# A short-convolution trunk on one core: the seventh small product behind product f, the convolution behind the addition of the sixth, w_out's sums and the small products' operands at other places

## The chip, the cores and the metric

The kernel runs on one core of a Trainium2 chip. The metric is device time in microseconds (us); the median of the runs is compared. The engines named below are PE (matmul), DVE (the vector engine), ACT (the scalar engine), POOL (GpSimd) and SP, whose queue issues nearly all DMAs. Each engine works through its own queue in the order in which the program names its instructions, and waits at the head of that queue until what it needs has been signalled.

## The reference

With DEPTH = 1 only layer 0 runs, the gated short convolution. For x of 1024 positions by 1024 channels:

```
u = rms_norm(x, pre_norm)
z, bg, cg, v = split(u @ w_in, 4)        # w_in: 1024 x 8192, each part 2048 wide
y = bg * causal_dwconv(cg * v, conv_w) * silu(z)     # 3 taps
out = x + rms_norm(y @ w_out, post_norm)             # w_out: 2048 x 1024
```

All of it is float32.

## The kernel before

The kernel computes y transposed, 128 channels of the 2048 at a time: 16 chunks c. A chunk is two pairs of column blocks of w_in: the even pair p = 2c holds (cg, v), the odd pair p = 2c + 1 holds (z, bg). A pair is computed by Strassen's method in a variant of seven products, named a to g, on halves of the 1024 rows of w_in and halves of the 1024 positions. Each product is 12 matmuls of 128 x 128 by 128 x 512: four blocks of rows, and three matmuls for each, because a float32 operand is split into a high part (a cast on ACT, L154) and a low part (a subtraction on DVE, L155), and high by low, low by high and high by high are added. `split_w` makes the two parts of one weight operand. The operands that are sums of weight blocks (c, d, e, f) come from POOL (`add_s`, L142 to L150).

The products a, c, d and g of a pair add into one PSUM bank x; between them the bank is read: by a copy on ACT (`snap`, L196, after a, c and e), or by an addition on DVE into the copy (L215 after d, L220 after f). The next product into the same bank must wait for the read of the one before.

From chunk 2 (DEEP) on, product b of the even and the odd pair is merged with the same method once more: b is made of seven small products a' to g', six matmuls of 128 x 256 each (L684 to L686). a', c', d' and g' share one bank, e' and f' another, and each small product is read by an addition on DVE (`deep_after`, L695). The first four belong to the even pair's stretch and f', d', g' to the odd pair's. Their position operands (c', d', e', g') are sums of blocks of product b's operand; POOL makes them once (`deep_parts`, L614 to L624, called after product f of pair 2) and `deep_split` makes their high and low parts on ACT and DVE. Their weight operands come from `deep_sums` on POOL and `deep_prep`.

The order of the program is one list of slots (L738 to L753): for an odd pair c, f', e, d', d, g', f, a of the next pair, g. For each slot PE's matmuls are issued, then `prepare` issues the splits of those weight operands whose slot begins within 7 us (LEAD) of this one's end by a fixed count of 2.72 us a product and 0.72 a small product, then `after` or `deep_after` issues the reads, then what is tied to the slot (L787 to L827).

The convolution of a chunk needs both halves of cg * v in the tile gpad: the second half is a POOL product after f of the even pair (L225), the first half is a DVE product after the last small product of the even row, f' (`start_conv`, L236). `conv` is a scaled copy on ACT over 1024 positions (L581) and two multiply-adds on DVE (L583). Its output cv is multiplied by the gates: after d (POOL, L217, then L223 after f) and after g (DVE, L229 and L230), which needs the SiLU of z on ACT (L779 after g', L222 after f). `y_done` then stores the chunk to DRAM.

The output projection is a Strassen product as well. Its operands that are sums are made during the first part and stored to DRAM: those of y by `add_y` (DVE, after d of an even pair), those of w_out by `add_t`: four subtractions and four stores, for blocks j = 0 to 6 on DVE in the even pairs 4 to 16, and for j = 7 on POOL in pair 17 (`TODO`, L735). `fetch_t` issues their loads after product c of the same pair. All loads and stores go through SP's queue in program order.

All working tiles of 128 x 512 float32 are pages of one pool of 36.

Of the kernel before, what the change touches and what calls it, by code (L numbers as in the profile page):

```python
# [16 lines left out]
DEEP = 2  # L17
# [4 lines left out]
def kernel(  # L22
# [16 lines left out]
    nc = tc.nc  # L39
# [5 lines left out]
    NC = CI // P  # L45
# [25 lines left out]
    def page(name, dtype=F32, shape=(HB,)):  # L71

        return pages.tile([P, *shape], dtype, tag="pg", name=name, bufs=PAGES)
# [58 lines left out]
    def block(p, n, k):  # L132
        return flat(raws[p, n, k])

    def add_s(p, kinds):

        if p >= len(PAIRS):
            return
        for i in kinds:
            if i == "d":  # L140
                t = block(p, 1, 0)
                nc.gpsimd.tensor_sub(t, block(p, 0, 0), t)  # L142
            else:
                t = page(f"s{i}_{p}")
                if i == "e":
                    nc.gpsimd.tensor_add(t, block(p, 1, 0), block(p, 1, 1))  # L146
                elif i == "c":
                    nc.gpsimd.tensor_sub(t, sums[p, "e"], block(p, 0, 0))  # L148
                else:
                    nc.gpsimd.tensor_sub(t, block(p, 0, 1), sums[p, "c"])  # L150
            sums[p, i] = t

    def split(src, hi, lo):
        nc.scalar.copy(hi, src)  # L154
        nc.vector.tensor_sub(lo, src, hi.bitcast(F32))  # L155
# [21 lines left out]
    def product(p, i, ks=None):  # L177

        w = wt[p, i]
        which = {"b": "y", "e": "v", "f": "v"}.get(i, "x")  # L180
        first = i in "abe"
        if first and (p, which) not in banks:
            banks[p, which] = bank(f"p{which}_{p}")
        ps = banks[p, which]
        for k in range(KH) if ks is None else ks:
            hi, lo = (h[:, k * P : (k + 1) * P] for h in w)
            last = k == KH - 1
            nc.tensor.matmul(ps, lo, UH[i][:, k], start=first and k == 0, stop=False, skip_group_check=True)  # L188
            nc.tensor.matmul(ps, hi, UL[i][:, k], start=False, stop=False, skip_group_check=True)  # L189
            nc.tensor.matmul(ps, hi, UH[i][:, k], start=False, stop=last, skip_group_check=True)  # L190
# [44 lines left out]
    def start_conv(c):  # L235
        nc.vector.tensor_mul(gpad[:, TAPS - 1 : TAPS - 1 + HB], banks[2 * c, "x"], sn[2 * c, "a"])  # L236
        conv(c)
# [8 lines left out]
    def fetch_s(c):  # L246

        if c >= CH:
            ts = [page(f"s{e}_{c}") for e in (0, 1)]
            for e in (0, 1):  # L250
                nc.sync.dma_start(ts[e], y_d[:, c - CH, e * HB : (e + 1) * HB])
            done[c] = done[c], *ts
# [19 lines left out]
    def fetch_t(j):  # L272

        ts[j] = [page(f"t{n}_{j}") for n in range(4)]
        for n, t in enumerate(ts[j]):
            nc.sync.dma_start(t, wov[:, j + n // 2 * CH, n % 2 * HB : (n % 2 + 1) * HB])

    def add_t(j, eng):

        t = ts.pop(j)  # L280
        eng.tensor_sub(t[1], t[1], t[0])
        eng.tensor_sub(t[3], t[3], t[1])
        eng.tensor_sub(t[0], t[3], t[0])
        eng.tensor_sub(t[2], t[2], t[3])
        for n in range(4):
            nc.sync.dma_start(t_d[:, n, j], t[n])
# [341 lines left out]
    def deep_split(i):  # L628

        k0, l0 = DEEP_U[i]  # L630
        ls = slice(l0, l0 + HH)
        if i != "e'":
            deep[i] = [tmp.tile([P, KQ, HH], F32R, tag="ub", name=f"u{i[0]}{h}_deep", bufs=6) for h in "hl"]
        for k in range(KQ):
            if i == "e'":
                hi, lo = UH["b"][:, k, ls], UL["b"][:, k, ls]
            else:
                hi, lo = (t[:, k] for t in deep[i])
            split(deep[k0 + k][:, ls], hi, lo)
# [29 lines left out]
    def deep_product(c, i):  # L669

        n, off = DEEP_W[i]
        which = {"b'": "y'", "e'": "v'", "f'": "v'"}.get(i, "x'")
        first = i in ("a'", "b'", "e'")
        if first:
            banks[c, which] = bank(f"p{which[0]}2_{c}")
        ps = banks[c, which][:, :HH]
        for k in range(KQ):
            hi, lo = (h[:, off + k * P : off + (k + 1) * P] for h in deep_w[c, n])
            if i in deep:
                uh, ul = (t[:, k] for t in deep[i])  # L680
            else:
                kk, l0 = {"a'": (k, 0), "b'": (k + KQ, 0), "e'": (k, HH), "f'": (k + KQ, HH)}[i]
                uh, ul = (u["b"][:, kk, l0 : l0 + HH] for u in (UH, UL))
            nc.tensor.matmul(ps, lo, uh, start=first and k == 0, stop=False, skip_group_check=True)  # L684
            nc.tensor.matmul(ps, hi, ul, start=False, stop=False, skip_group_check=True)
            nc.tensor.matmul(ps, hi, uh, start=False, stop=k == KQ - 1, skip_group_check=True)  # L686
# [5 lines left out]
    def deep_after(c, i):  # L692
        which, row, half = DEEP_C[i]
        t = sn[2 * c + row, "a"][:, half * HH : (half + 1) * HH]
        nc.vector.tensor_add(t, banks[c, which][:, :HH], t)  # L695
        if i == "f'":
            start_conv(c)


# [35 lines left out]
    TODO = {p: p // 2 - 2 for p in range(4, 4 + 2 * CH - 2, 2)}  # L735
# [3 lines left out]
    for p in range(2, len(PAIRS)):  # L739
        q = p + 1  # L740
        more = p // 2 >= DEEP
        sub = {"c": "a'", "e": "b'", "f": "c'", "a": "e'"} if p % 2 == 0 else {"c": "f'", "e": "d'", "d": "g'"}
        for i in "cedf":
            slots.append((i, p))
            if more and i in sub:
                slots.append((sub[i], p // 2))
        if q <= END:
            slots.append(("a", q))
            if more and p % 2 == 0:
                slots.append((sub["a"], p // 2))  # L750
            if q // 2 < DEEP:
                slots.append(("b", q))
        slots.append(("g", p))  # L753


    at, t = [], 0.0
# [6 lines left out]
    def prepare(n):  # L763
        while ready[0] < len(slots) and at[ready[0]] < at[n + 1] + LEAD:
            i, p = slots[ready[0]]
            if i[1:]:
                deep_prep(p, i)
            elif (p, i) not in wt:
                split_w(p, i)
            ready[0] += 1  # L770

    first_chunk("")
    for n, (i, p) in enumerate(slots):
        if i[1:]:
            deep_product(p, i)
            prepare(n)
            deep_after(p, i)
            if i == "g'":
                nc.scalar.activation(sn[2 * p + 1, "a"], sn[2 * p + 1, "a"], AF.Silu)  # L779
            continue  # L780
        product(p, i)
        prepare(n)
        after(p, i)
        q, prev = p + 1, p // 2 - 1
        if p == 2:
            first_chunk(i)
        if i == "c":  # L787
            if p % 2 and p // 2 < DEEP:
                nc.scalar.activation(sn[p, "a"], sn[p, "a"], AF.Silu)
            if p in TODO:  # L790
                fetch_t(TODO[p])
            if p % 2 == 0 and p > 2:
                fetch_s(prev)
            if p % 2 == 0 and p // 2 >= DEEP:
                deep_sums(p // 2, 1)
        elif i == "e":
            add_s(q, "ec")
        elif i == "d":
            if p + 2 <= END:
                fetch(p + 2)  # L800
            add_s(q, "d")
            if p % 2 == 0 and p > 2:
                add_y(prev)
        elif i == "f":
            add_s(q, "f")
            if p == 2:
                add_y(0)
            if p == 2 and DEEP < NC:
                deep_parts()
        elif i == "g":  # L810
            if p in TODO:
                add_t(TODO[p], nc.gpsimd if p % 2 else nc.vector)
            if p % 2 and q <= END and q // 2 >= DEEP:
                deep_sums(q // 2, 0)
            if p == 2 and DEEP < NC:
                deep_split("c'")
                deep_split("e'")
        if p == 3 and DEEP < NC:
            if i == "c":
                deep_split("d'")  # L820
            elif i == "e":
                deep_split("g'")
        if p == END - 1 and i in "cd":
            fetch_unit()
        if p == END and i in "acdg":
            split_unit()
            fetch_unit()  # L827
# [153 lines left out]
```

## Time and profile before

| | |
|---|---|
| median of 3 runs | 816.36 us (816.34 to 816.61) |
| profiled execution | 817.24 us |
| its span (first to last instruction) | 815.3 us |
| mean granted clock of PE | 0.994 |
| busy: PE, DVE, POOL, ACT | 785.2, 645.3, 356.8, 333.1 us |

In the timeline a row is: start, length, engine, line, operation, the tiles written and read, and in square brackets the idle time of the engine before it and what ended it. Lengths of successive rows of one engine can overlap a little, since instructions are pipelined; the steps from start to start are what adds up. A matmul's row is longer than its step for the same reason. In the list of waits a row gives total, number and longest. In the windows a row is the stretch, its length, the busy time and the number of instructions of PE, PEld (the weight loads), DVE, ACT and POOL, then the granted clock, the share of DMA and GB/s.

### The profile page before, as it was taken

How to read it: one execution, taken by the hardware profiler on the slowest of the kernel's cores; microseconds unless marked ns; L12 is line 12 of the kernel's file. 1: busy time of each engine (PE TensorE's matmuls, PEld its weight loads, DVE VectorE, ACT ScalarE, POOL GpSimd, SP SyncE). 2: the span in 40 equal slices, each digit the busy share in tenths (PEclk: the TensorE clock that was granted, in tenths of full speed). 3: DMA queues.
4: the chain of work that ended last, by engine and by line, in shares of the span. 5: the costliest groups of instructions: out<-in, count | busy, mean ns of one | idle time of the engine just before them, and what ended most of it. 6: DMA issues, size and time to landing. Idle time of an engine off the chain costs nothing.

```text
span 815.3 us, 10812 instructions
## 1 busy us (share of the span) xinstructions
PE 785.2 (96%) x3746; PEld 655.8 (80%) x3746; DVE 645.3 (79%) x835; ACT 333.1 (41%) x612; POOL 356.8 (44%) x265
## 2 busy tenths in 40 slices
PE   9999699999999999999999999999999899999996
PEld 8888588878787878787878887888888788888885
DVE  6899788888797979797888878787879867744766
ACT  7555332333333342433342434242433547544541
POOL 2616873646373737464754637373736100000020
PEclk9999899999999999999999999999999999999999
DMA  9111333434343434344705142332324659974037
GB/s 331 33 52 43 99 124 123 141 106 142 104 142 104 142 105 143 104 149 148 246 21 174 46 148 75 120 103 91 104 91 138 210 168 387 405 257 139 0 99 263
DMA packets 108325, 114.50 MB, mean 140 GB/s; under 512 B 6584, under 2 KB 72176, under 8 KB 108272
## 3 DMA queue, kind: packets, MB, share of 16 engines
q1 hardware_dynamic: 108256, 113.82, 42.1%
q8 instruction: 29, 0.48, 0.2%
q14 instruction: 24, 0.20, 0.1%
q10 hardware_dynamic: 16, 0.00, 0.0%
HBM read 84.44 MB, written 29.36 MB: 140 GB/s over the span
## 4 chain that ended last, share of the span: by engine, by line
PE 62%; DVE 16%; issue 7%; ACT 5%; DMA 5%; POOL 4%; SPq 1%; DVEq 0%; POOLq 0%; ACTq 0%
PE px L188 9%; PE px L189 9%; PE px L190 9%; PE pv L188 4%; PE pv L189 4%; PE pv L190 4%; PE po_x L858 3%; PE po_x L859 3%; PE po_x L857 3%; DVE cv L583 2%; PE po_v L858 2%; PE po_v L859 2%; PE po_v L857 2%; PE px L684 1%; ACT cv L581 1%
## 5 line engine op out<-in xcount | busy, mean ns | idle before, releaser
L217 POOL TENSOR_TENSOR sne<-sne,cv 128x512 f32<-128x512 f32 x15 | 20.1, 1343 | 161.4 <-DVE sne L215 161.4
L899 POOL TENSOR_TENSOR acc<-acc,xr 128x512 f32<-128x512 f32 x4 | 6.3, 1586 | 134.9 <-DVE acc L898 133.4
L196 ACT COPY snc<-px 128x512 f32<-128x512 f32 x31 | 18.2, 586 | 102.9 <-PE px L190 102.9
L583 DVE SCALAR_TENSOR_TENSOR cv<-gpad,cw,cv 128x1024 f32<-128x1024 f32 x32 | 42.0, 1313 | 19.0 <-ACT cv L581 18.4
L188 PE MATMUL px<-u_d,wdl 128*128 128x512 f32 x124 | 49.7, 401 | 6.7 <-ACT snc L196 6.7
L196 ACT COPY sna<-px 128x512 f32<-128x512 f32 x30 | 17.5, 584 | 93.5 <-PE px L190 93.5
L150 POOL TENSOR_TENSOR sf<-raw,sc 128x512 f32<-128x512 f32 x31 | 53.5, 1725 | 0.0
L155 DVE TENSOR_TENSOR wel<-se,weh 128x512 fp32r<-128x512 f32 x31 | 52.9, 1706 | 0.0
L146 POOL TENSOR_TENSOR se<-raw,raw 128x512 f32<-128x512 f32 x31 | 52.0, 1677 | 0.9 <-ACT sna L196 0.5
L148 POOL TENSOR_TENSOR sc<-se,raw 128x512 f32<-128x512 f32 x31 | 49.7, 1602 | 3.0 <-POOL se L146 0.7
L189 PE MATMUL px<-u_d,wdh 128*128 128x512 f32 x124 | 49.5, 399 | 0.0
L190 PE MATMUL px<-u_d,wdh 128*128 128x512 f32 x124 | 49.0, 395 | 0.0
L188 PE MATMUL pv<-u_e,wel 128*128 128x512 f32 x124 | 48.6, 392 | 0.0
L189 PE MATMUL pv<-u_e,weh 128*128 128x512 f32 x124 | 48.6, 392 | 0.0
L188 PE MATMUL pv<-u_f,wfl 128*128 128x512 f32 x124 | 48.6, 392 | 0.0
L188 PE MATMUL px<-u_a,wal 128*128 128x512 f32 x124 | 48.5, 391 | 0.0
L189 PE MATMUL pv<-u_f,wfh 128*128 128x512 f32 x124 | 48.4, 391 | 0.0
L225 POOL TENSOR_TENSOR gpad<-snc,sne 128x512 f32<-128x512 f32 x15 | 19.7, 1314 | 65.6 <-DVE snc L220 65.6
L188 PE MATMUL px<-u_g,wgl 128*128 128x512 f32 x124 | 48.4, 390 | 0.0
L189 PE MATMUL px<-u_a,wah 128*128 128x512 f32 x124 | 48.4, 390 | 0.0
L188 PE MATMUL px<-u_c,wcl 128*128 128x512 f32 x124 | 48.4, 390 | 0.1
L189 PE MATMUL px<-u_g,wgh 128*128 128x512 f32 x124 | 48.4, 390 | 0.0
(374 smaller groups left out, 2570.0 us busy)
## 6 DMA issues: line engine op xcount, KB each, us to landing
raw<-in_sc_w_in SPq DMA_DIRECT2D x128, 256.0 KB, 4.1
y_d<-cv SPq DMA_DIRECT2D x16, 512.0 KB, 3.0
s_d<-s SPq DMA_DIRECT2D x32, 256.0 KB, 2.6
t<-in_sc_w_out SPq DMA_DIRECT2D x32, 256.0 KB, 4.4
t_d<-t SPq DMA_DIRECT2D x32, 256.0 KB, 2.4
s<-y_d SPq DMA_DIRECT2D x16, 256.0 KB, 3.8
xr<-in_x SPq DMA_DIRECT2D x16, 256.0 KB, 4.8
xa<-in_x SPq DMA_DIRECT2D x4, 512.0 KB, 5.1
```

What stands on the lines that cost most here:

```text
L146: nc.gpsimd.tensor_add(t, block(p, 1, 0), block(p, 1, 1))
L148: nc.gpsimd.tensor_sub(t, sums[p, "e"], block(p, 0, 0))
L150: nc.gpsimd.tensor_sub(t, block(p, 0, 1), sums[p, "c"])
L155: nc.vector.tensor_sub(lo, src, hi.bitcast(F32))
L188: nc.tensor.matmul(ps, lo, UH[i][:, k], start=first and k == 0, stop=False, skip_group_check=True)
L189: nc.tensor.matmul(ps, hi, UL[i][:, k], start=False, stop=False, skip_group_check=True)
L190: nc.tensor.matmul(ps, hi, UH[i][:, k], start=False, stop=last, skip_group_check=True)
L196: nc.scalar.copy(t, banks[p, "v" if i == "e" else "x"])
L583: nc.vector.scalar_tensor_tensor(cv, gpad[:, j : j + L], tap(c, j), cv, op0=ALU.mult, op1=ALU.add)
L857: nc.tensor.matmul(ps, lo, u[:, 0, k], start=first, stop=False, skip_group_check=True)
L858: nc.tensor.matmul(ps, hi, u[:, 1, k], start=False, stop=False, skip_group_check=True)
L859: nc.tensor.matmul(ps, hi, u[:, 0, k], start=False, stop=last, skip_group_check=True)
```

## The change

No instruction is added or removed; four things stand elsewhere in the program's order.

1. The slot of g' in an odd pair stands behind product f and not behind product d. The order is c, f', e, d', d, f, g', a, g. The SiLU that follows g' moves with it, and the planner's count of due times changes accordingly: the split of w_f for the odd pair is issued one slot earlier, that of g's small operand one slot later.
2. `start_conv`, with the convolution behind it, is issued after the addition of d' and not after that of f'.
3. `add_t` is issued after product d (behind `add_s` and ahead of `add_y`) and not after product g. On DVE this holds for pairs 4 to 16; on POOL, for pair 17, it stands ahead of L223 and the sum of w_f.
4. The four calls of `deep_split` move: c' and e' stood after g of pair 2, d' after c and g' after e of pair 3. Now c' stands after d and d' after f of pair 3, e' after a of pair 4 and g' after g of pair 3 (in this order).

```diff
@@ deep_after
-        if i == "f'":
+        if i == "d'":
             start_conv(c)
@@ the slots
-        sub = {"c": "a'", "e": "b'", "f": "c'", "a": "e'"} if p % 2 == 0 else {"c": "f'", "e": "d'", "d": "g'"}
+        sub = {"c": "a'", "e": "b'", "f": "c'", "a": "e'"} if p % 2 == 0 else {"c": "f'", "e": "d'", "f": "g'"}
...
+    UNDER = {("d", 3): "c'", ("f", 3): "d'", ("a", 4): "e'", ("g", 3): "g'"}
@@ the loop over the slots
             add_s(q, "d")
+            if p in TODO:
+                add_t(TODO[p], nc.gpsimd if p % 2 else nc.vector)
             if p % 2 == 0 and p > 2:
                 add_y(prev)
...
         elif i == "g":
-            if p in TODO:
-                add_t(TODO[p], nc.gpsimd if p % 2 else nc.vector)
             if p % 2 and q <= END and q // 2 >= DEEP:
                 deep_sums(q // 2, 0)
-            if p == 2 and DEEP < NC:
-                deep_split("c'")
-                deep_split("e'")
-        if p == 3 and DEEP < NC:
-            if i == "c":
-                deep_split("d'")
-            elif i == "e":
-                deep_split("g'")
+        if DEEP < NC and (i, p) in UNDER:
+            deep_split(UNDER[i, p])
```

## The prediction

> **What bounds the kernel now.** I read the page first, then PE's waits, then one steady chunk on all engines, then the places that differ from it. PE is busy for 96% of the span at full clock, with one dip of the clock in the fifth slice:
>
> ```profile
> PE 785.2 (96%) x3746; PEld 655.8 (80%) x3746; DVE 645.3 (79%) x835; ACT 333.1 (41%) x612; POOL 356.8 (44%) x265
> PEclk9999899999999999999999999999999999999999
> ```
>
> So a new order can win back PE's gaps and nothing else. PE's waits (us in total, times, longest) name two kinds, and a chunk of two pairs, here one with w_out's sums and one without, lasts 38.90 us either way:
>
> ```profile
> PE px L684 <- DVE sna L695: 15.1, 14, 3.3
> PE px L188 <- ACT snc L196: 6.7, 1, 6.7
> 121.83:160.73 38.90, 38.05 (x188) 31.91 (x187) 33.13 (x38) 13.90 (x25) 20.95 (x15) 1.00 0.39 125
> 432.00:470.90 38.90, 38.06 (x188) 31.94 (x187) 31.95 (x36) 13.92 (x25) 20.87 (x15) 1.00 0.32 102
> ```
>
> The columns of the last two are length, then PE, PEld, DVE, ACT, POOL busy: DVE has 33.1 of 38.9 us filled. L684 is the first matmul of a small product; 14 waits are one for each chunk from c = 2 to 15. The timeline of chunk 10 shows which:
>
> ```profile
> 444.79 0.28 PE L684 MATMUL pv<-u_b,dw2l 128*128 128x256 f32 x1
> 451.47 0.39 PE L190 MATMUL px<-u_d,wdh 128*128 128x512 f32 x1
> 452.70 0.38 PE L684 MATMUL px<-ugh_deep,dw 128*128 128x256 f32 x1 [0.84 <-DVE sna L695]
> 452.92 0.28 PE L685 MATMUL px<-ugl_deep,dw 128*128 128x256 f32 x1
> 447.19 0.69 DVE L236 TENSOR_TENSOR gpad<-px,sna 128x512 f32<-128x512 f32 x1
> 447.91 1.16 ACT L581 ACTIVATE cv<-gpad,cw 128x1024 f32<-128x1024 f32 x1 [1.82 <-DVE gpad L236]
> 449.10 2.60 DVE L583 SCALAR_TENSOR_TENSOR cv<-gpad,cw,cv 128x1024 f32<-128x1024 f32 x2 [1.22 <-ACT cv L581]
> 451.62 0.69 DVE L155 TENSOR_TENSOR wal<-raw,wah 128x512 fp32r<-128x512 f32 x1
> 452.23 0.42 DVE L695 TENSOR_TENSOR sna<-px,sna 128x256 f32<-128x256 f32 x1
> 453.76 0.42 DVE L695 TENSOR_TENSOR sna<-px,sna 128x256 f32<-128x256 f32 x1
> 453.92 1.29 POOL L217 TENSOR_TENSOR sne<-sne,cv 128x512 f32<-128x512 f32 x1 [10.87 <-DVE sne L215]
> 456.94 0.68 DVE L220 TENSOR_TENSOR snc<-pv,snc 128x512 f32<-128x512 f32 x1
> 458.83 1.45 DVE L155 TENSOR_TENSOR dw0l<-raw,dw0h 128x512 fp32r<-128x512 f32 x1 [1.21 <-ACT dw0h L154]
> 459.23 0.59 ACT L196 COPY sna<-px 128x512 f32<-128x512 f32 x1
> 471.53 0.69 DVE L215 TENSOR_TENSOR sne<-px,sne 128x512 f32<-128x512 f32 x1 [0.31 <-PE px L190]
> 479.02 0.41 DVE L695 TENSOR_TENSOR sna<-pv,sna 128x256 f32<-128x256 f32 x1
> ```
>
> g' adds into the bank that d' has filled and DVE must have read (L695, 452.23). That read stands in DVE's queue behind the whole convolution (L236, ACT's 1.16, two L583), which began after f'. PE steps by 0.23 per matmul of 512 columns, 2.72 a product, 0.70 a small one (six of 0.117); from 451.47 to 452.70 it loses 1.00, and 0.10 more before L685: 1.10.
>
> **Steps 1 and 2: g' behind f, convolution behind d'.** The two go together, no instruction is added or lost. d' ends where d begins, at 451.70 - 2.72 = 448.98. Now DVE reads it at once (448.98), then L236 at 449.4, ACT's cv at 450.15, L583 from 451.35 to 453.87. Behind it in DVE's queue come w_g's low part (0.6), L215 at 454.5 (POOL's L217, now 453.92, goes to 455.3), w_c's low part (1.4 beside POOL), L220 at 456.5 and the read of g' at 457.1. PE goes d to 451.70, f to 454.42, g' to 455.12, a to 457.84, g to 460.56. g' needs the read of d' (done at 449.4): the wait is gone. g needs L215, done at 455.2, at 457.84. What is late next is ACT: SiLU of snc waits for L220 (457.2), SiLU of sna for the read of g', then two casts (0.53 each, the copy's 0.59 less the overlap) and the snapshot of a at 459.3 to 459.9, which c of the next pair needs at 460.56: 0.65 to spare. DVE's next low part, dw0l, starts at 458.9 against 458.83 now. So all behind it stays where it is on DVE's clock while PE is 1.1 earlier; the 0.31 that L215 waited at 471.53 was room for that, and the splits are a product ahead of PE. The planner's shift (w_f's split a slot earlier, that of g's small operand a slot later for a product 2.7 later) and the pages (sna of the even pair held two slots longer, w_out's tiles freed sooner) cost nothing that PE's two kinds of waits would show. Price 0, cover 0.65 at the snapshot; if that goes, c waits by the excess. Gain 1.10 in each of the 12 regular chunks: 13.2.
>
> **Step 3: w_out's sums behind d instead of g (on DVE in the seven even pairs 4 to 16).** Rows of chunk 7; the last, from the list of DMA issues, ends with the median time to landing:
>
> ```profile
> 308.77 2.22 SPq L276 DMA_DIRECT2D t<-in_sc_w_out  x4
> 314.88 0.69 DVE L215 TENSOR_TENSOR sne<-px,sne 128x512 f32<-128x512 f32 x1 [0.35 <-PE px L190]
> 323.52 1.77 DVE L281 TENSOR_TENSOR t<-t,t 128x512 f32<-128x512 f32 x1
> t<-in_sc_w_out SPq DMA_DIRECT2D x32, 256.0 KB, 4.4
> ```
>
> The four subtractions (now from 323.52, the first at 1.77 beside POOL) come to stand between L215 and add_y, 2.8 at 0.69 each (L236's time for the same shape), since POOL is idle at that place. No wait is new to DVE, but the loads must have landed sooner: issued 308.77 to 310.99, they land by 315.4; L215, without its wait of 0.35, ends at 315.2, the first subtraction needs only the first two tiles, the second (316) the fourth. Price 0; bounds -1 (the 1.77 falls to 0.69) and +1 a chunk (late landing). Queued behind are add_y, w_c's low part, L220, c', w_e and the read of e' that f' needs. In chunk 10 that read is done at 479.43, while f', 38.9 after 444.79 and 1.1 earlier, comes at 482.6: 3.2 to spare; a chunk with sums has 2.8 + 0.7 where chunk 10 has three subtractions of add_y (2.1), so 1.4 less: 1.8 to spare. On SP the four stores only pass add_y's one store, whose data comes after theirs anyhow; the next loads of weights come two products later.
>
> **Step 4: the eighth sum, on POOL in pair 17.** It moves ahead of L223 and of the sum of w_f for pair 18. Rows of now, and of the last chunk for step 5:
>
> ```profile
> 382.51 1.74 POOL L281 TENSOR_TENSOR t<-t,t 128x512 f32<-128x512 f32 x1
> 387.61 1.74 POOL L284 TENSOR_TENSOR t<-t,t 128x512 f32<-128x512 f32 x1
> 411.75 0.39 PE L190 MATMUL px<-u_d,wdh 128*128 128x512 f32 x1
> 413.81 0.38 PE L684 MATMUL px<-ugh_deep,dw 128*128 128x256 f32 x1 [1.67 <-DVE sna L695]
> 645.96 0.39 PE L190 MATMUL px<-u_d,wdh 128*128 128x512 f32 x1
> 649.60 0.39 PE L684 MATMUL px<-ugh_deep,dw 128*128 128x256 f32 x1 [3.25 <-DVE sna L695]
> 640.62 2.50 DVE L155 TENSOR_TENSOR oy_a<-ry_a,oy_a 128x512 fp32r<-128x512 f32 x4 [2.25 <-ACT oy_a L154]
> ```
>
> It takes 6.84 (382.51 to 389.35). In chunk 10's clock: L217 at 455.3, two operations of 1.29 to 457.8, the sums to 464.7, L223 to 466.0, w_f's sum (1.74 like L281) to 467.7. ACT stands at w_f's cast; behind it is the snapshot of c, which d of pair 18 needs. Cast and snapshot end at 468.85; d could start at 460.56 + 2 x 2.72 + 2 x 0.70 = 467.4. A new wait of 1.45 (0.8 to 2). The t_d stores now hold y_d in SP's queue until 464.7, but y_d waits for L223 anyhow. What falls away is chunk 9's wait, which came from the late sums of pair 18: 2.06 - 0.23 + 0.10 = 1.93. Gain 0.5.
>
> **Step 5: the last chunk.** g' loses 3.64 - 0.23 + 0.10 = 3.5 there, because DVE stands at oy_a until 643.1 and the convolution comes after it. Now oy_a is followed by the read of f', two low parts (1.0), the read of d' at 644.4, L236, cv, L583 to 649.3, L215 to 650.0. No a stands between g' and g, so g, due at 646.19 + 2.72 + 0.70 = 649.6, waits 0.4. Gain 3.1.
>
> **Step 6: the small products' operands.** Rows around deep_parts:
>
> ```profile
> 89.99 0.39 PE L190 MATMUL pv<-u_e,weh 128*128 128x512 f32 x1
> 97.09 0.79 PE L188 MATMUL px<-u_d,wdl 128*128 128x512 f32 x1 [6.71 <-ACT snc L196]
> 102.28 0.40 PE L188 MATMUL pv<-u_f,wfl 128*128 128x512 f32 x1
> 95.02 0.40 ACT L154 CAST uch_deep<-deep 128x256 fp32r<-128x256 f32 x1 [2.74 <-POOL deep L622]
> 96.47 0.57 ACT L196 COPY snc<-px 128x512 f32<-128x512 f32 x1
> 82.42 6.96 POOL L618 TENSOR_TENSOR deep<-u_b 128x512 f32<-128x512 f32 x4
> 98.16 1.35 POOL L148 TENSOR_TENSOR sc<-se,raw 128x512 f32<-128x512 f32 x1
> ```
>
> ACT waits for POOL's parts with the casts (95.02), and the snapshot of c in pair 3 stands behind them: d, due at 90.22, starts at 97.09, 6.87 lost, and then runs slow (5.19 instead of 2.72): 9.34 in all. With the casts behind d the snapshot follows c's end (87.5) at once, and d, f, a, g run from 90.22 to 101.10. POOL's queue is unchanged: w_c's sum for pair 4 is done at 99.5 now, and later by up to 2 because DVE's low parts of w_f, w_a, w_g, now early, run beside it: I take 100.6. ACT has w_c's cast waiting for it, and behind that in its queue everything up to the snapshot of a in pair 4: cast 0.5, low part and L220 on DVE 1.4 to 2.2, SiLU 0.5, two casts of d' 0.6, two of weights 1.1, snapshot 0.6: 4.7 to 5.5. So c of pair 4 starts at 105.8 instead of 101.1: a wait of 4.7 (3.2 to 6). DVE is late too: L220 at 102.3, then what takes 456.94 to 479.43 in chunk 10, less 0.31, plus 1.4 of sums, plus six halves of operands at 0.5: the read of e' ends at 128.9, and f', due 7 x 2.72 + 4 x 0.70 = 21.8 after c, at 127.6, waits 1.2. New waits 5.9, gain 3.4.
>
> A stop of 3.41 (649.60) left the clock whole, the stop of 6.87 halved it; 4.7 lies between, and I leave the clock whole. By the Trainium skill (TensorE: Matmul & The Clock Gate, Part 1) an idle window of about 3.4 us is enough to halve it, which would add the 2.4 us again; the trace agrees for the long stop and shows nothing for 4.7.
>
> **The sum.** 13.2 + 0 + 0.5 + 3.1 + 3.4 = 20.2. The profiled execution took 817.24 (span 815.3, 1.9 around it), 0.9 over the median of 816.36. 817.24 - 20.2 = 797.0, against the median 796.2.
>
> **The rivals.**
> - The clock still halves at c of pair 4: +2.4, 798.6. For it the long stop, against it the 3.41.
> - The operands' move brings nothing: POOL's sums are the bound, c of pair 4 starts at 107.1 and f' waits more, 9.3 again: 799.6. For it: POOL works nearly without a gap from 82.42 to 99.5.
> - Waits of 0.5 to 1 in the seven chunks with sums (late landing, DVE's backlog before f'): 800 to 803.
> - The wait only moves to c of the next pair, through the snapshot of a: if DVE's chain from L583 to the read of g' is 1.75 longer (0.65 + 1.1), the 13.2 are back: 809.4. For it the small margin; against it POOL's 10.87 of idling before L217, so nothing slows DVE there.
> - Slower: DVE stands at the first subtraction of w_out for loads that haven't landed, in seven chunks. It decides from 20.2 / 7 = 2.9 a chunk, over the 1.8 of margin: 4.7 late, a landing after 9 instead of 4.4. At 6 late: 7 x 4.2 = 29 lost, 825. Nothing in the DMA list speaks for it.
>
> **Chances.** Forecast 0.40 (own range 793.5 to 798), clock 0.20, operands nothing 0.10, sums 0.15, moved wait 0.10, slower 0.05. A measurement tells 0.2% (1.6 us). The range 792.5 to 806 leaves out the moved wait, the slower case and a little below: 2 in 10. Below, all waits gone would be 13.2 + 1.9 + 3.5 + 9.3 = 28, 788. Faster 0.93, within 0.2% 0.01, slower 0.06, where a hundredth stands for what I haven't seen.
>
> **What would show it.** The waits of PE on L695 at g' gone, chunks of 37.8; convolution's L236 right behind the read of d'; PE's d in pair 3 right behind e; a PE wait on ACT's snapshot of a at c of pair 4, one at f' behind it, one on the snapshot of c in pair 18, a short one at the last g. Wrong would be PE waits at c in every chunk, or DVE waiting on DMA at L281.

## The result, and the profile after

The changed kernel takes 797.31 us (median of 5 runs, 797.08 to 797.89), the kernel before 816.61 beside it (5 runs, 816.34 to 819.32): a ratio of 0.9756, 95% interval 0.974 to 0.9773. The profiled execution took 797.1, with a span of 795.3 against 815.3.

The busy line and the clock line of the page after:

```profile
PE 781.3 (98%) x3746; PEld 656.7 (83%) x3746; DVE 602.8 (76%) x835; ACT 335.9 (42%) x612; POOL 371.6 (47%) x265
PEclk9999989999999999999999999999999999999999
```

Its waits of PE (us in total, times, longest), the two on snapshots:

```profile
PE px L188 <- ACT sna L196: 4.5, 1, 4.5
PE px L188 <- ACT snc L196: 1.1, 1, 1.1
```

No wait of PE on L695 is left, where there were 14. The two new waits on ACT's snapshots are at c of pair 4 and at d of pair 18, both shown below. The dip of the clock is still there, one slice later: it belongs to the first of them. (The list of waits counts idle time alone. Where a stop is given below with its place, it is the step between two matmuls less the usual 0.23 or 0.12, and so a little longer: 4.68 for this 4.5.)

The windows of the two chunks that the prediction showed (length, then busy PE, PEld, DVE, ACT, POOL), and the stretch of the dip:

```profile
126.00:163.80 37.80, 37.80 (x188) 32.03 (x187) 30.70 (x39) 14.22 (x25) 22.96 (x16) 1.00 0.41 133
432.00:469.80 37.80, 37.80 (x188) 32.02 (x187) 28.66 (x36) 14.11 (x25) 22.02 (x16) 1.00 0.33 105
104.20:111.00 6.80, 5.45 (x13) 4.29 (x14) 6.80 (x7) 3.57 (x9) 6.36 (x7) 0.50 0.00 0
```

A chunk lasts 37.80 instead of 38.90, PE fills it, and 1.10 is what it lost at g'. The granted clock was 0.50 for 6.8 us from 104.2 on (called the half clock below). Rows of the timeline of chunk 10 show the new order:

```profile
438.17 0.42 DVE L695 TENSOR_TENSOR sna<-px,sna 128x256 f32<-128x256 f32 x1 [2.02 <-PE px L686]
438.51 0.68 DVE L236 TENSOR_TENSOR gpad<-px,sna 128x512 f32<-128x512 f32 x1
440.41 2.61 DVE L583 SCALAR_TENSOR_TENSOR cv<-gpad,cw,cv 128x1024 f32<-128x1024 f32 x2 [1.22 <-ACT cv L581]
443.43 0.28 PE L684 MATMUL px<-ugh_deep,dw 128*128 128x256 f32 x1
444.14 0.68 DVE L155 TENSOR_TENSOR wcl<-sc,wch 128x512 fp32r<-128x512 f32 x1
444.30 1.68 POOL L217 TENSOR_TENSOR sne<-sne,cv 128x512 f32<-128x512 f32 x1 [12.18 <-DVE sne L215]
445.34 0.42 DVE L695 TENSOR_TENSOR sna<-px,sna 128x256 f32<-128x256 f32 x1
447.54 0.58 ACT L196 COPY sna<-px 128x512 f32<-128x512 f32 x1
449.60 0.39 PE L188 MATMUL px<-u_c,wcl 128*128 128x512 f32 x1
```

DVE now waits for PE at the read of d' (438.17), not PE for DVE: g' (443.43) comes 4.8 after that read has ended. The snapshot of a ends at 448.12, and c of the next pair starts at 449.60 without a wait: 1.5 to spare.

The transition from the first chunks to those with small products (pairs 3 and 4), pair 18, and the last chunk, in rows of the same timeline:

```profile
100.37 0.62 ACT L154 CAST wch<-sc 128x512 fp32r<-128x512 f32 x1 [3.89 <-POOL sc L148]
105.56 0.80 PE L188 MATMUL px<-u_c,wcl 128*128 128x512 f32 x1 [4.52 <-ACT sna L196]
...
110.84 0.36 PE L684 MATMUL px<-u_b,dw0l 128*128 128x256 f32 x1
...
370.24 1.81 POOL L281 TENSOR_TENSOR t<-t,t 128x512 f32<-128x512 f32 x1
379.67 0.62 ACT L154 CAST wfh<-sf 128x512 fp32r<-128x512 f32 x1 [7.98 <-POOL sf L150]
380.83 0.50 PE L188 MATMUL px<-u_d,wdl 128*128 128x512 f32 x1 [1.13 <-ACT snc L196]
...
632.92 0.28 PE L686 MATMUL px<-ugh_deep,dw 128*128 128x256 f32 x1
633.23 0.50 PE L188 MATMUL px<-u_g,wgl 128*128 128x512 f32 x1
```

The stop of 6.87 at d of pair 3 is gone; c of pair 4 stops for 4.68 in its place, and then runs from 105.56 to 110.84, 5.28 instead of 2.72: 2.56 for the half clock. Pair 18 has its new wait (1.29 against PE's step), the last g stands for 0.20.

Of the 20.0 of the spans, 13.2 are the regular waits (12 x 1.10), 1.93 chunk 9's wait less 1.29 at pair 18, 3.3 the last chunk (3.5 less 0.20), 2.1 the transition (9.34 less 4.68 and 2.56): 19.2. The other 0.8 I can't put in one place; 0.23 of it was there ahead of everything that the change touches, when c of pair 3 began (84.78 before, 84.55 after).

### The profile page after: what moved, and what is told of

The parts are those of the page before. It is cut to its first block, busy times and chain, and to the rows that moved or that the text cites. A ratio compares the mean times of both kernels' runs of the same rounds, so it can differ in the third digit from the quotient of the medians.

```text
span 795.3 us, 10869 instructions
## 1 busy us (share of the span) xinstructions
PE 781.3 (98%) x3746; PEld 656.7 (83%) x3746; DVE 602.8 (76%) x835; ACT 335.9 (42%) x612; POOL 371.6 (47%) x265
## 4 chain that ended last, share of the span: by engine, by line
PE 82%; issue 2%; POOL 2%; DVE 0%; ACT 0%; DVEq 0%; POOLq 0%; ACTq 0%
PE px L188 12%; PE px L189 12%; PE px L190 12%; PE pv L188 6%; PE pv L189 6%; PE pv L190 6%; PE po_x L855 4%; PE po_x L856 4%; PE po_x L854 4%; PE po_v L855 2%; PE po_v L856 2%; PE po_v L854 2%; PE px L684 2%; PE px L686 2%; PE px L685 2%
## 5 line engine op out<-in xcount | busy, mean ns | idle before, releaser
L217 POOL TENSOR_TENSOR sne<-sne,cv 128x512 f32<-128x512 f32 x15 | 24.7, 1646 | 161.4 <-DVE sne L215 145.7
L190 PE MATMUL px<-u_c,wch 128*128 128x512 f32 x124 | 49.2, 397 | 0.0
L189 PE MATMUL px<-u_c,wch 128*128 128x512 f32 x124 | 49.2, 397 | 0.0
L189 PE MATMUL px<-u_d,wdh 128*128 128x512 f32 x124 | 48.6, 392 | 0.0
L189 PE MATMUL px<-u_a,wah 128*128 128x512 f32 x124 | 48.6, 392 | 0.0
L189 PE MATMUL px<-u_g,wgh 128*128 128x512 f32 x124 | 48.4, 391 | 0.0
L190 PE MATMUL px<-u_a,wah 128*128 128x512 f32 x124 | 48.2, 389 | 0.0
L190 PE MATMUL px<-u_g,wgh 128*128 128x512 f32 x124 | 48.2, 389 | 0.0
L190 PE MATMUL px<-u_d,wdh 128*128 128x512 f32 x124 | 48.2, 389 | 0.0
```

Of the source, the lines that this page charges most:

```text
L217: nc.gpsimd.tensor_mul(t, t, cvs[c][:, HB:])
```

## The experiments

All ratios are against runs of the kernel before on the same chip, beside the run in question. There its medians were 817.65 to 819.3, so a ratio says more than a difference to 816.61. Which move brought what is read from the profiles, for the medians of two kernels on different chips differ by as much as the smaller effects.

### Which of the two moves does it: parts 1, 2, and both

Parts 1 and 2 of the change, and nothing else of it:

```diff
-... {"c": "f'", "e": "d'", "d": "g'"}
+... {"c": "f'", "e": "d'", "f": "g'"}
-        if i == "f'":
+        if i == "d'":
             start_conv(c)
```

> Only parts 1 and 2 of the change (g' behind f, convolution behind d'); w_out's sums stay behind g and the small products' operands stay where they were. Theory (the three gains are separate, as summed in the prediction): the 12 regular waits of 1.10, chunk 9's 1.93 and 3.1 of the last chunk's 3.5 go, the stop of 6.87 with its slow clock in pair 3 stays, no new wait in pair 18: 18.2 less, 798.2 against 816.4. Rival (the sums of w_out have to move too, since DVE's queue is too full behind g once the convolution is later): waits of 0.5 to 1 come back in seven chunks, 802 to 805.

Measured: 799.33 (799.18 to 800.27), ratio 0.976 [0.9739, 0.9781]; span 797.2. The regular waits are gone, the stop of 6.7 before d of pair 3 stays, and a wait of 1.03 is new at f of pair 18 (385.47), where the eighth sum still stands behind g.

Part 1 alone (only the line with the slots):

> Only part 1 (g' behind f), the convolution stays behind f'. Theory (the wait is DVE's late read of d', no more): that read ends about 452.6 in chunk 10's clock and g' comes at 454.4, so the regular waits go by this part alone; in the last chunk the read ends at 649.5 against g' at 648.9, a wait of 0.6. 13.2 + 1.9 + 2.9 = 18.0 less, 798.4. Rival (only both together help, because g' merely meets the next late read): at least half of the 13.2 stays, 805 or more.

Measured: 798.08 (797.39 to 798.89), ratio 0.9739 [0.9715, 0.9764]; span 797.1. Chunk 10 of this kernel by its window:

```profile
432.00:469.80 37.80, 37.80 (x188) 32.02 (x187) 29.73 (x36) 13.91 (x25) 21.21 (x16) 1.00 0.33 105
```

Rows of its timeline around g':

```profile
441.84 0.42 DVE L695 TENSOR_TENSOR sna<-px,sna 128x256 f32<-128x256 f32 x1
444.72 0.28 PE L684 MATMUL px<-ugh_deep,dw 128*128 128x256 f32 x1
448.37 0.59 ACT L196 COPY sna<-px 128x512 f32<-128x512 f32 x1 [0.53 <-PE px L190]
450.89 0.39 PE L188 MATMUL px<-u_c,wcl 128*128 128x512 f32 x1
```

The read of d' stands behind the whole convolution as before and ends at 442.26, but g' wants it a product later, at 444.72: 2.5 to spare. The snapshot of a waits for PE itself and ends 1.9 ahead of c. One line of the change brings 18.2 of the 20.0 of the span (815.3 to 797.1).

Part 2 alone (only `start_conv`, g' still behind d):

> Only part 2 (convolution behind d'), g' stays behind d. Theory (late read of d'): the read is done at 449.4 and g' comes at 451.7, so this part alone lifts the regular waits as well; last chunk: read at 644.8, no wait at g', a short one at g. 13.2 + 1.9 + 3.1 = 18.2 less, 798.2. Rival (DVE's late additions then hold up g or the next c): PE waits of 0.5 and more in every chunk, 804 or more.

Measured: 809.74 (809.06 to 810.48), ratio 0.9885 [0.9863, 0.9906]; span 808.4. My theory failed here and the rival held. PE's waits of this kernel:

```profile
PE px L188 <- ACT sna L196: 6.0, 13, 0.5
```

Its window of chunk 10:

```profile
432.00:470.54 38.54, 38.07 (x188) 31.91 (x187) 31.80 (x36) 14.21 (x25) 20.87 (x15) 1.00 0.32 102
```

Rows of its timeline from the read of g' to c of the next pair:

```profile
453.19 0.41 DVE L695 TENSOR_TENSOR sna<-px,sna 128x256 f32<-128x256 f32 x1
453.69 0.63 ACT L779 ACTIVATE sna<-sna 128x512 f32<-128x512 f32 x1 [3.76 <-DVE sna L695]
454.23 0.60 ACT L154 CAST wch<-sc 128x512 fp32r<-128x512 f32 x1
454.87 1.58 DVE L155 TENSOR_TENSOR wcl<-sc,wch 128x512 fp32r<-128x512 f32 x1 [1.27 <-ACT wch L154]
457.08 0.63 ACT L222 ACTIVATE snc<-snc 128x512 f32<-128x512 f32 x1 [2.25 <-DVE snc L220]
458.65 0.57 ACT L196 COPY sna<-px 128x512 f32<-128x512 f32 x1
459.28 0.50 PE L188 MATMUL px<-u_c,wcl 128*128 128x512 f32 x1 [0.47 <-ACT sna L196]
```

g' no longer waits, and c of the next pair does, in 13 chunks: 38.54 instead of 37.80. With g' ahead of f in the program, the SiLU of sna stands in ACT's queue ahead of w_c's cast and waits for DVE's read of g' (3.76 idle). w_c's low part, L220, the SiLU of snc and the snapshot of a follow one behind the other, and 0.62 of it shows at c. With g' behind f, the cast of w_c is ahead of that SiLU, and the chain falls apart. A further wait, of 1.82, is new at f of pair 18 (391.81). So the two moves do not share the gain: the first alone has 18.2 of the span, the second alone 6.9, because it passes more than half of the regular wait on (0.74 of 1.10 a chunk).

Parts 1, 3 and 4, that is the changed kernel with the convolution put back behind f':

```diff
-        if i == "d'":
+        if i == "f'":
             start_conv(c)
```

> The changed kernel with the convolution alone put back behind f'. Theory (g' behind f is what lifts the regular wait; the convolution's place is worth nothing beside it, or a little against it, since L215 and POOL's L217 come earlier without it): PE's regular chunks stay at 37.8 and the wait of 1.3 in pair 18 shrinks, as POOL reaches the eighth sum about 1.4 earlier; the last g' waits 0.5 instead of 0.2 at g. 796.3 against 797.3. Rival (the convolution behind d' is needed once sums and operands have moved): a wait on DVE in the chunks, 799 or more.

Measured: 796.06 (794.89 to 796.61), ratio 0.9715 [0.9697, 0.9732]; span 794.7, 0.6 less than the changed kernel's, with a half clock of 6.8 us in both profiles. PE's waits in the chunks are the stop at c of pair 4 (4.70) and 0.53 at the last f; pair 18 has none:

```profile
365.74 1.67 POOL L217 TENSOR_TENSOR sne<-sne,cv 128x512 f32<-128x512 f32 x1 [8.99 <-DVE sne L215]
368.64 1.30 POOL L281 TENSOR_TENSOR t<-t,t 128x512 f32<-128x512 f32 x1
378.55 0.58 ACT L196 COPY snc<-px 128x512 f32<-128x512 f32 x1
```

L217, and behind it the eighth sum (370.24 in the changed kernel), start 1.6 earlier, so that the snapshot of c is there in time. Beside part 1, the convolution's move gains nothing in the regular chunks, costs 1.29 in pair 18, and saves 0.3 at the end.

### The sums

Part 3 alone (all of `add_t` behind d):

```diff
             add_s(q, "d")
+            if p in TODO:
+                add_t(TODO[p], nc.gpsimd if p % 2 else nc.vector)
...
         elif i == "g":
-            if p in TODO:
-                add_t(TODO[p], nc.gpsimd if p % 2 else nc.vector)
```

> Only part 3 (w_out's sums behind d), everything else as before. Theory (on DVE the seven sums are free at either place; the eighth, on POOL, holds up w_f's sum and so the snapshot of c in pair 18): a new wait of about 1.3 at d of pair 18, chunk 9's extra 0.8 at g' goes, the rest stays: +0.5, 816.9. Rival (the loads of w_out's blocks land too late for DVE): a wait of DVE on DMA at L281 in seven chunks and 818 or more.

Measured: 817.88 (median of 10, 815.01 to 818.9), ratio 0.9997 [0.9984, 1.001]. No chunk with sums has a new wait of PE, and DVE waits for no load at the sums. Chunk 9's wait at g' fell from 1.83 to 1.01, and the wait that I expected in pair 18 did not appear. The 0.8 is below what the times can tell, the more so since the clock was halved behind the last g' in the profiled execution (taken up with the clock below).

The changed kernel with the eighth sum back at g of pair 17:

```diff
-            if p in TODO:
-                add_t(TODO[p], nc.gpsimd if p % 2 else nc.vector)
+            if p in TODO and p % 2 == 0:
+                add_t(TODO[p], nc.vector)
...
         elif i == "g":
+            if p in TODO and p % 2:
+                add_t(TODO[p], nc.gpsimd)
```

> The changed kernel with the eighth sum alone put back behind g of pair 17. Theory: the wait of 1.29 at d of pair 18 goes and nothing comes in its place, because the read of d' no longer stands behind the late small operands of pair 18: 796.0 against 797.3. Rival (the late sums of the small products' weights hold PE at c' or f' instead): no gain, 797.3 or more.

Measured: 796.32 (795.48 to 797.53), ratio 0.9745 [0.9731, 0.976]. The wait at d of pair 18 is gone, but my theory that nothing comes in its place failed: another stands at its f, for the eighth sum is now ahead of the small operand's sum on POOL, whose cast ACT waits for:

```profile
380.52 0.62 ACT L154 CAST dw1h<-ds 128x512 fp32r<-128x512 f32 x1 [5.46 <-POOL ds L648]
381.56 0.58 ACT L196 COPY sne<-pv 128x512 f32<-128x512 f32 x1
382.19 0.50 PE L188 MATMUL pv<-u_f,wfl 128*128 128x512 f32 x1 [0.88 <-ACT sne L196]
```

1.04 there against 1.29: the place of the eighth sum is worth 0.25. That the time came near the 796.0 that I expected is luck: the half clock lasted 3.41 in this profile and not 6.8, so that c of pair 4 took 4.39 instead of 5.28.

### The operands and the clock

Part 4 alone (the dictionary `UNDER` and its call instead of the four calls):

```diff
+    UNDER = {("d", 3): "c'", ("f", 3): "d'", ("a", 4): "e'", ("g", 3): "g'"}
...
+        if DEEP < NC and (i, p) in UNDER:
+            deep_split(UNDER[i, p])
```

> Only part 4 (the small products' operands elsewhere). Theory (the stop moves from d of pair 3 to c of pair 4, shortens from 6.87 to 4.7, and the clock is halved after both): the waits at g' stay; 6.87 + 2.47 becomes 4.7 + 2.6, 2.0 less, 814.4. Rival (with the convolution's order of before DVE's backlog after the stop costs PE a second wait at f'): gain 0 to 0.8, 815.6 to 816.4.

Measured: 815.89 (median of 10; four from 813.6 to 814.05, six from 815.81 to 817.11), ratio 0.9962 [0.9944, 0.9979]. The stop sits at c of pair 4, 4.67 long. The profiled execution is one of the six. Its windows behind c of pair 4 and behind the last g':

```profile
106.59:110.00 3.41, 3.41 (x10) 2.64 (x9) 3.41 (x4) 1.88 (x5) 3.33 (x4) 0.50 0.00 0
645.90:652.70 6.80, 5.76 (x17) 4.80 (x18) 5.40 (x9) 1.10 (x2) 1.66 (x1) 0.50 0.00 0
```

Here the half clock after the 4.67 lasted half as long as in the changed kernel; and the stop of 3.41 (3.25 of it idle) at the last g', which had left the clock whole in the profile of the kernel before, halved it. The same in the profile of part 3 alone, by its timeline:

```profile
648.31 0.58 PE L684 MATMUL px<-ugh_deep,dw 128*128 128x256 f32 x1 [3.25 <-DVE sna L695]
```

Its window there:

```profile
647.60:654.30 6.70, 5.99 (x17) 5.03 (x18) 5.07 (x8) 0.77 (x2) 1.66 (x1) 0.50 0.00 0
```

And the window of that place in the kernel before:

```profile
649.60:655.00 5.40, 5.40 (x27) 4.58 (x28) 4.98 (x7) 0.99 (x2) 1.67 (x1) 1.00 0.00 0
```

So one stop of 3.25 idle goes both ways, and 2 to 3 us hang on it. That would divide the six from the four of part 4 alone, and it fits that the kernel before, with that stop, spreads over 3 us and the changed kernel, without it, over 0.8. The mean granted clock on record for every run agrees: it is 0.996 in each of the four and 0.992 or 0.993 in each of the six, and 6.8 us at half clock lower the mean over 815 us by 0.004. At which place the clock was halved in runs without a profile is argued, not shown.

To see whether idling is what halves the clock, the stop in the changed kernel was filled with 20 matmuls whose results are thrown away:

```diff
         product(p, i)
+        if (i, p) == ("g", 3):
+            dummy = bank("pdummy")
+            for _ in range(20):
+                nc.tensor.matmul(dummy, wt[3, "g"][0][:, :P], UH["a"][:, 0], start=True, stop=True, ...)
```

> The changed kernel with 20 matmuls of 128 x 512 into a spare bank behind g of pair 3, 4.5 us of work that fits in the stop of 4.7 before c of pair 4 and is thrown away. Theory (the clock is halved because PE stands idle in that stop): the clock stays whole, c of pair 4 runs at 0.23 a matmul instead of 0.43, 2.6 less; DVE has that much less time, so f' of chunk 2 waits 1.2: 795.9. Rival (the low clock there does not come from the idle time): no gain, 797.3 or, with matmuls that run over, up to 798.

Measured: 796.11 (796.01 to 796.47), ratio 0.9742 [0.9728, 0.9757]; span 794.7. The clock line of its page:

```profile
PEclk9999999999999999999999999999999999999999
```

Two rows of its timeline:

```profile
106.11 0.50 PE L188 MATMUL px<-u_c,wcl 128*128 128x512 f32 x1
117.06 0.47 PE L188 MATMUL pv<-u_f,wfl 128*128 128x512 f32 x1 [1.01 <-DVE wfl L155]
```

The clock stays whole though c starts no earlier (106.11); over all four runs the mean granted clock is 0.997 or 0.998, against 0.993 to 0.995 in the five of the changed kernel. A wait of 1.17 appears behind it, at f of pair 4, because DVE has w_f's low part ready too late. With the half clock PE had given DVE the time for it. So the half clock costs 2.56, but only 1.2 to 1.4 net (2.56 less 1.17; by the spans 0.6, and 0.55 by which c starts later here).

The kernel before with its two stops filled in the same manner, 28 matmuls behind e of pair 3 and 14 behind d of pair 31:

> The kernel before with matmuls into a spare bank in its two long stops, 28 behind e of pair 3 (6.4 us of the 6.87) and 14 behind d of pair 31 (3.2 of the 3.41); their result is thrown away. Theory (idle time of PE halves the clock, in the first stop always, in the second in some executions): no half clock in the profile, 2.4 less than the lower runs of before, and none of the runs 2 to 4 us above the others: 813.6 to 814.5 each. Rival (the spread of the runs of before, 816.3 to 820.5, has nothing to do with the second stop): the runs of this kernel spread as far.

Measured: 821.04 (median of 10, 820.33 to 821.56), ratio 1.0029 [1.0018, 1.004]. The first half did as expected: from the start of d of pair 3 to that of f it took 3.15 instead of 5.19, at full clock. The second half spoilt the test. The added matmuls read u_a and, as I read the program, held its buffer, so that the output's operand took another one; ACT came to wait for PE. ACT's row in the timeline of this kernel:

```profile
637.50 2.18 ACT L154 CAST ou_a<-ru_a 128x512 fp32r<-128x512 f32 x4 [5.59 <-PE px L190]
```

And the new entry among its waits of PE:

```profile
PE pv L684 <- DVE sna L695: 3.6, 1, 3.6
```

A new stop of 3.73 at f' of the last chunk halved the clock from 640.0 to 646.8. How much of the spread of the kernel before comes from its last stop is thus not settled by this run.

### Taking the stop itself away

ACT's wait in the transition is for POOL (`sc`, 3.89 in the row at 100.37): the sum of w_c for pair 4 stands behind `deep_parts`. Put ahead of its subtractions, with the operands spread over later products:

```diff
@@ deep_parts, between its two loops
+        add_s(4, "ec")
@@
-    UNDER = {("d", 3): "c'", ("f", 3): "d'", ("a", 4): "e'", ("g", 3): "g'"}
+    UNDER = {("g", 3): "c'", ("f", 4): "e'", ("c", 5): "d'", ("e", 5): "g'"}
@@
         elif i == "e":
-            add_s(q, "ec")
+            if p != 3:
+                add_s(q, "ec")
```

> The changed kernel with POOL's first two sums for pair 4 between the additions and the subtractions of deep_parts, and the small products' operands later: c' after g of pair 3, e' after f of pair 4, d' after c and g' after e of pair 5. Theory (the stop at c of pair 4 is POOL's late sum for w_c, held in ACT's queue ahead of the snapshot of a): that sum is done at about 93, the stop of 4.68 and its slow clock of 2.6 go: 7.3 less, 790.0, or 791 to 792 if DVE's backlog costs a wait at f'. Rival (POOL's whole load is the bound there, so a later sum stops PE as long): 795 to 797.

Measured: 797.2 (796.59 to 797.51), ratio 0.9754 [0.9739, 0.9768]. c of pair 4 starts at 100.79 without a wait, but e' now stops for 3.60 and the clock halves behind it (119.4 to 126.2):

```profile
120.31 0.58 PE L686 MATMUL pv<-u_b,dw1h 128*128 128x256 f32 x1 [3.44 <-DVE u_b L155]
```

Neither theory had this place: the operands of e', issued behind f of pair 4, stand on DVE behind w_out's sums and the additions of y, and come at 119.84.

The kernel before with part 1, POOL's sums first, and all four operand splits behind a of pair 4:

```diff
+        if (i, p) == ("a", 4) and DEEP < NC:
+            for j in ("e'", "c'", "d'", "g'"):
+                deep_split(j)
```

> The kernel before with part 1 alone (g' behind f), POOL's first two sums for pair 4 ahead of the subtractions of deep_parts, and all four sets of small operands after a of pair 4, behind its snapshot, where DVE stood idle for 4.5 us in the run that had those sums first. Theory: no stop in pairs 3 to 5 and no slow clock; what stays is about 0.5 at the last g': 18 of the first part, 9.3 of the stop, 789.3. Rival (DVE's backlog in the first chunk with small products stops PE at e' again): 792 to 795.

Measured: 792.82 (792.7 to 793.42), ratio 0.9681 [0.9667, 0.9695]; span 791.1. The clock is whole, and two waits are left in the transition (2.33 at d and 1.24 at f of pair 4). The rival was right in the time and in that DVE is the cause, not in the place, which was e': eight halves of operands at once stand ahead of w_d's low part on DVE.

```profile
110.45 0.47 PE L188 MATMUL px<-u_d,wdl 128*128 128x512 f32 x1 [2.28 <-DVE wdl L155]
```

The same with only e' and c' behind a of pair 4:

```diff
+    UNDER = {("a", 4): ("e'", "c'"), ("c", 5): ("d'",), ("e", 5): ("g'",)}
```

> As the kernel with POOL's two sums first and all operands after a of pair 4, but only those of e' and c' there; d' comes after c and g' after e of pair 5, where DVE has room. Theory (the waits of 2.33 at d and 1.24 at f of pair 4 came from DVE, which made four operands beside POOL ahead of w_d's and w_f's low parts, two of them long before they were needed): w_d's low part starts at about 105 instead of 109.1, both waits go: 3.5 less, 789.3. Rival (POOL's later sums for w_d and w_f are the bound there): no more than 1 less, 791.8 or more.

Measured: 791.39 (791.15 to 791.59), ratio 0.9668 [0.9645, 0.9691]; span 789.5. Its transition by the window:

```profile
84.00:126.00 42.00, 41.57 (x197) 34.63 (x196) 37.62 (x38) 17.06 (x32) 37.59 (x28) 1.00 0.32 98
```

And the stop at d of pair 4 in its timeline:

```profile
108.23 0.50 PE L188 MATMUL px<-u_d,wdl 128*128 128x512 f32 x1 [0.43 <-ACT snc L196]
```

PE works 41.57 of the 42.00 us at full clock. In the chunks no wait is over 0.6 any more. The time is 2.1 over the 789.3 that I expected; five waits of 0.4 to 0.6 are left or new, 2.4 in all. It is the fastest version that ran, about 5.9 below the changed kernel (on different chips; by the ratios 0.9668 against 0.9756). It has neither the convolution's move nor that of w_out's sums; adding the sums' move to it wasn't tried.

## Why the prediction was right

I had 796.2 us, within 792.5 to 806; measured 797.31. The gain in the profile was 20.0 against my 20.2. That it is so close is in part luck: step 6 fell short by 1.3, steps 4 and 5 brought 0.3 more than forecast, and 0.8 came that I can't place. The medians differ by more, because I subtracted from a median that lay 0.9 under the profiled execution, and the changed kernel's lies 0.2 over its own.

- **Steps 1 and 2, 13.2:** right in size (37.80 a chunk). Wrong was that the two go together: part 1 alone has all of it. The row that said so was quoted: the read of d' ended at 452.65, and behind f g' comes at 454.42 even with the convolution where it was. The margin at the snapshot was 1.5, not 0.65, mostly since I took 1.4 for w_c's low part beside POOL and it took 0.68. The rival of the wait moving to c is what part 2 alone does, though through ACT's queue and not through DVE's length.
- **Step 3, 0:** right. The loads land in time; only in the first chunk with sums did DVE wait 0.30 for one.
- **Step 4, gain 0.5:** right in sum (1.93 less 1.29, I had 1.45), mostly wrong in the cause. Moving the sums alone does take the 0.8 by which chunk 9's wait was longer than the others, but the whole wait goes with part 1 already: part 1 alone has no wait on L695. And the new wait in pair 18 comes from the convolution's move: without it there is none, with the eighth sum at either place, and with it there is one at either place (1.29 at d, 1.03 at f).
- **Step 5, gain 3.1:** 3.3; g waits 0.20, not 0.4. This too comes with part 1.
- **Step 6, gain 3.4:** this is where the prediction failed. c of pair 4 started at 105.56 (I had 105.8) after a stop of 4.68 (4.7): right. "I leave the clock whole" was wrong, and cost 2.56. That was my rival of 0.20. By the Trainium skill (TensorE: Matmul & The Clock Gate, Part 1) an idle window of about 3.4 us halves the clock; the trace agrees, with 0.50 from 104.2 to 111.0. My ground, that 3.41 had left it whole, was a single instance; the same stop halved it in two other profiles. The wait of 1.2 at f' of chunk 2 for the read of e' appeared in no profile, not even with the stop filled and the clock whole. The 1.17 that came there is another wait, at f of pair 4 for w_f's low part, and its like size is chance. Net 2.1 instead of 3.4.

So the change is nearly all one line, g' behind f; the operands' move adds some 2, the sums' nothing that can be told, and the convolution's move a small loss (1.29 at pair 18 less 0.3 at the end).

## What to carry to other kernels

When a change moves two things together, work out each of them alone: compare when the late result is ready now with when its user would come in the new order, and see whose queue the other move lengthens. Price a stop near 3 us or longer with and without a half clock behind it, and do not take one row in which the clock held for a rule. Where an engine stands for another's result, put that result's producer earlier rather than its users later: pushing the users back moved the stop (4.68, then 3.60), and putting POOL's sum first, with the operands in small groups, took it away.

## What the runs showed of the hardware

**The clock.** Stops of 3.60 and longer (3.60, 3.73, 4.67 to 4.70, 6.87 to 6.89) halved the clock in every profile that has one, the idle 3.25 before the last g' in two of three. In two of the four runs with the convolution put back behind f' the mean granted clock is 0.997, as in kernels without a dip, so a stop of 4.70 may not always cost it; no profile shows those two. The half clock lasted one of two lengths: 3.41 (part 4 alone, 106.59 to 110.00; the eighth sum at g, 105.33 to 108.75) or 6.8 (the changed kernel, 104.18 to 111.00).

By the Trainium skill (TensorE: Matmul & The Clock Gate, Part 1) the window of about 3.4 us runs freely, and a kernel's start doesn't reset it. The traces agree, and they tell more. Within a profile the half clocks begin whole multiples of 3.413 apart: 106.59 and 645.89 in part 4 alone (158 times), 94.60 and 647.56 in part 3 alone (162 times). So what counts is how a stop lies in these stretches. Of the stop of 3.41, 2.36 lay in one stretch in part 4 alone and 2.67 in part 3 alone, and the clock halved at that stretch's end. In the kernel before (stretches counted on from its half clock at 95.32) it was split into 2.1 and 1.3, and the clock stayed whole. A limit between 2.1 and 2.4 is an estimate from these three profiles. The length fits too: the half clock ended after 3.41 in the two places where PE stood idle for at most 0.05 of them, and after 6.8 wherever it stood idle for 0.7 or more.

**DVE beside POOL.** Of two operations that overlap, it isn't always DVE's that takes longer. In chunk 10 of the changed kernel w_c's low part took 0.68 while POOL's L217, which began beside it, took 1.68 (before: 1.29); with only the convolution moved the same low part took 1.58, beside POOL's L142 of 1.29. In both places the one that began first kept its time (DVE at 444.14 ahead of POOL at 444.30; POOL at 454.61 ahead of DVE at 454.87). Two places don't make it a rule.
